# Folded attention: both masked halves on VectorE, the scaling of all four heads on ScalarE

## The chip, the cores and the metric

The kernel runs on one core of one Trainium2 chip. The core has a matrix engine (TensorE, in the profile PE for matmuls and PEld for its weight loads), VectorE (DVE), ScalarE (ACT), GpSimd (POOL), and SyncE (SP), which issues the DMA transfers. The metric is the device time of one execution in microseconds, as the median of several runs. Each engine works through its own instructions in the order of the program; engines wait for each other on semaphores.

## The reference

One decoder layer on a sequence of 1024 positions and a width of 1024, in float32. Part of it is a sliding-window attention with 16 query heads on 2 key/value heads and a learned sink per head, which enters the softmax but has no value:

```python
qb = q.reshape(B, N, C, Hkv, G, d)          # N = 8 blocks of C = 128, G = 8, d = 64
kb = jnp.concatenate([kp[:, :-1], kp[:, 1:]], axis=2)   # the block before, and this one
scores = jnp.einsum('bnqhgd,bnkhd->bnhgqk', qb, kb) * (d ** -0.5)
mask = (rel >= 0) & (rel < WINDOW) & (key_pos >= 0)     # WINDOW = 128
scores = jnp.where(mask, scores, -1e30)
m = jnp.maximum(jnp.max(scores, axis=-1, keepdims=True), sink)
e = jnp.exp(scores - m)
probs = e / (jnp.sum(e, axis=-1, keepdims=True) + jnp.exp(sink - m))
out = jnp.einsum('bnhgqk,bnkhd->bnqhgd', probs, vb)
```

Around it stand the combined input projection, a chunkwise retention with four heads, two sigmoid gates, an output projection and a SwiGLU block of 2816 columns, with RMS norms between.

## The kernel before, in words

Matmuls keep nearly float32 precision by splitting each operand into a high part (`h`) and the rest (`l`) and adding three products (hi·hi, hi·lo, lo·hi): ScalarE writes the high part, VectorE the difference.

The attention is *folded*. With a window of 128, query i of a block needs the keys after i in the block before and the keys up to i in its own: together always 128. So the two halves of scores are laid over each other in one 128×128 matrix, chosen by a mask. The values then need two products: the folded probabilities times one of the two value blocks, and the probabilities under the mask times the difference of the two value blocks (`vdf`).

The work is cut into 32 units: four groups g of four query heads, times eight blocks b. For a unit, `u_scores` makes the score matmuls (L477, L478, into PSUM tiles `s`), copies and chooses the halves (L482 on ScalarE, L483 on VectorE), takes the row minimum (L485; scores are negated), exponentiates on ScalarE with a row sum (L493; each has a second, short instruction that reads the sum), takes the reciprocal (L496, VectorE) and multiplies the probabilities of heads 1 and 3 on ScalarE (L499) and of heads 0 and 2 on VectorE (L501). GpSimd copies the sink column into the score tile (L469). `u_transpose` transposes the four heads on TensorE (L509, `pT`), writes the high part `ph` (L511, ScalarE) and the low part `pl` (L512, VectorE), and, for every block but the first of a group, multiplies both by the mask on GpSimd (L519, `qh` and `ql`). `u_values` runs the value matmuls on ph, pl, qh and ql (L530), brings the two halves of the heads together in `tm` (L533 and L534 on ScalarE, L535 and L536 on VectorE) and splits the result into hi and lo (L538, L539).

`ph`, `pl`, `qh` and `ql` have one buffer each (`bufs=1`), the score tile two.

Between units, dense matmuls fill TensorE: the query projections of the next group (`quad_q`, L159 to L161 with `aq`, with splits of weights in L419 and L420, and the rotation on VectorE and ScalarE in L427 to L446) and gate columns (`gate`, the same lines with `acc_g`, weights split in L132 and L135, tanh in L545). The loop hands out 8 steps of three matmuls a unit:

```python
            if i > 0:
                u_transpose(i - 1)
            if i < NU:
                u_scores(i)
            fl.step((i + 1) * left // (NU + 1) - i * left // (NU + 1))
            if i > 0:
                u_values(i - 1)
```

The order in which instructions really stand is not that of this text. A scheduler of the framework takes the instructions as they are traced, with its own assumed cost for each on its engine, and sets the order of every engine's queue from that. A changed engine or cost therefore moves the rows of all engines in the stage. What follows the attention (retention, output, SwiGLU) is not touched in the code.

## Time and profile before

| | us |
|---|---|
| Median of three runs (1582.39 to 1582.92) | 1582.56 |
| Profiled execution, its own time | 1584.13 |
| Its span, first to last instruction | 1582.3 |
| TensorE busy (matmuls) | 1555.2, 98% |
| VectorE busy | 1013.4, 64% |
| ScalarE busy | 719.6, 45% |
| GpSimd busy | 452.8, 29% |
| Mean granted TensorE clock | 0.996 |

Folded attention with its fill stands between about 95 and 342 us of the span. A row of the table by stage gives the stage, its length, then the busy time of PE, PEld, DVE, ACT and POOL with the number of instructions, then the granted clock as a share of the full one, the share of DMA engines in use, and GB/s. A row of the waits reads: engine, tile and line that waited, the engine, tile and line that released it, total us, times, longest. A row of the timeline gives start, duration, engine, line, operation, out<-in, and in brackets the idle time of the engine just before and who ended it. Matmuls are pipelined and their shown ends are modelled, so that consecutive rows overlap; the distance of two starts is what a matmul costs.

### The profile page before, as it was taken

What the parts mean: (1) busy time and instruction counts of PE and PEld (TensorE: products, weight loads), DVE (VectorE), ACT (ScalarE), POOL (GpSimd) and SP (SyncE); (2) the same over time, 40 slices, a digit from 0 to 9 for tenths busy, and PEclk for the clock granted to TensorE, in tenths of its full rate; (3) what the DMA queues carried; (4) which work ended last, traced back from release to release, by engine and by line L of the source; (5) the groups of instructions that cost most, each with busy time, mean ns of one, the idle gap of its engine ahead of it and who ended that gap; (6) DMA issues with size and microseconds to landing.
All of it is one profiled execution on the core that took longest, in us unless ns stands there. A gap on an engine that the chain in (4) does not pass through costs nothing.

```text
span 1582.3 us, 20602 instructions
## 1 busy us (share of the span) xinstructions
PE 1555.2 (98%) x7323; PEld 1288.0 (81%) x7323; DVE 1013.4 (64%) x1676; ACT 719.6 (45%) x1492; POOL 452.8 (29%) x376
## 2 busy tenths in 40 slices
PE   9998899999999999999999999999999999999998
PEld 8876777888888888888888888888888888888886
DVE  6458869677758663688656879544444444678656
ACT  6356777753333334544323366333333333344445
POOL 2013334320035541000021122655555555100001
PEclk9999899999999999999999999999999999999999
DMA  6563466350274543755455502333333333762233
GB/s 214 160 166 94 158 220 195 101 170 31 74 256 143 154 150 133 272 194 174 142 202 185 210 1 72 108 106 110 109 102 100 102 109 109 280 256 83 99 102 125
DMA packets 152581, 228.43 MB, mean 144 GB/s; under 512 B 9307, under 2 KB 81821, under 8 KB 150942
## 3 DMA queue, kind: packets, MB, share of 16 engines
q1 hardware_dynamic: 152476, 227.10, 43.6%
q8 instruction: 58, 0.95, 0.2%
q14 instruction: 45, 0.37, 0.1%
q10 hardware_dynamic: 2, 0.00, 0.0%
HBM read 152.36 MB, written 69.99 MB: 141 GB/s over the span
## 4 chain that ended last, share of the span: by engine, by line
PE 89%; DVE 4%; ACT 4%; POOL 2%; issue 1%; DMA 1%; POOLq 0%; DVEq 0%; ACTq 0%; SPq 0%
PE fA L1549 15%; PE fB L1549 8%; PE dA L1851 7%; PE wA L873 7%; PE dxP L1851 6%; PE fC L1549 4%; PE wB L873 3%; PE wo L1383 3%; PE va L718 3%; PE acc_g L159 2%; PE acc_g L160 2%; PE acc_g L161 2%; PE woP L1383 2%; PE vP L718 2%; PE acc_ba L159 2%; PE acc_ba L160 2%
## 5 line engine op out<-in xcount | busy, mean ns | idle before, releaser
L1851 PE MATMUL dA<-dwP,daP 128*128 128x512 f32 x528 | 120.6, 389 | 0.0
L1851 PEld LDWEIGHTS dA<-dwP,daP 128*128 128x128 f32 x528 | 99.1, 188 | 20.7 <-DVE dwP L135 0.2
L1851 PE MATMUL dxP<-dwP,daP 128*128 128x512 f32 x396 | 90.2, 389 | 0.0
L1851 PEld LDWEIGHTS dxP<-dwP,daP 128*128 128x128 f32 x396 | 74.3, 188 | 15.4
L159 PE MATMUL acc_g<-h,wh_g 128*128 128x512 f32 x192 | 77.2, 402 | 1.4 <-ACT wh_g L132 1.4
L160 PE MATMUL acc_g<-h,wh_g 128*128 128x512 f32 x192 | 76.2, 397 | 0.0
L161 PE MATMUL acc_g<-h,wl_g 128*128 128x512 f32 x192 | 75.8, 396 | 0.0
L1624 POOL TENSOR_TENSOR xf<-xf 128x512 f32<-128x512 f32 x40 | 62.4, 1561 | 30.7 <-issue 28.9
L469 POOL COPY sc<-nsink 128x4 f32<-128x4 f32 x32 | 11.5, 359 | 191.1 <-PE pT L509 157.8
L1555 POOL TENSOR_TENSOR xf<-xf 128x512 f32<-128x512 f32 x33 | 47.3, 1434 | 59.0 <-ACT xf L1557 26.9
L1756 POOL TENSOR_TENSOR rs_f<-tot,mhalf 128x1 f32<-128x1 f32 x8 | 4.8, 606 | 205.4 <-DVE tot L1753 205.4
L493 ACT ACTIVATE sc<-sc,nm 128x129 f32<-128x129 f32 x128 | 50.4, 396 | 26.6 <-DVE nm L485 20.7
L135 DVE TENSOR_TENSOR dwP<-wd,dwP 128x512 fp32r<-128x512 f32 x77 | 52.9, 687 | 5.3 <-ACT dwP L132 5.3
L1038 POOL TENSOR_TENSOR grs<-gve,mhalf 128x2 f32<-128x2 f32 x16 | 11.2, 701 | 145.5 <-DVE gve L1036 145.5
L587 POOL TENSOR_TENSOR wr_f<-wr_f 128x512 f32<-128x512 f32 x20 | 30.6, 1532 | 76.8 <-DVE t_10P L135 8.6
L132 ACT CAST dwP<-wd 128x512 fp32r<-128x512 f32 x77 | 47.4, 616 | 9.3 <-PE dA L1851 7.1
L587 POOL TENSOR_TENSOR wr_wp<-wr_wp 128x512 f32<-128x512 f32 x10 | 16.1, 1611 | 121.7 <-DVE w0P L135 103.6
L159 PE MATMUL acc_bb<-ay,wh_bb 128*128 128x512 f32 x128 | 50.9, 399 | 0.0
L132 ACT CAST daP<-daP 128x512 fp32r<-128x512 f32 x42 | 26.0, 621 | 54.2 <-PE dxP L1851 26.7
L159 PE MATMUL aq<-h,wh_aq 128*128 128x512 f32 x128 | 50.4, 394 | 0.0
L160 PE MATMUL acc_bb<-ay,wh_bb 128*128 128x512 f32 x128 | 50.3, 393 | 0.0
L160 PE MATMUL aq<-h,wh_aq 128*128 128x512 f32 x128 | 50.3, 393 | 0.0
(841 smaller groups left out, 4485.7 us busy)
## 6 DMA issues: line engine op xcount, KB each, us to landing
act_d<-xf SPq DMA_DIRECT2D x77, 256.0 KB, 2.1
daP<-act_d SPq DMA_DIRECT2D x21, 512.0 KB, 3.7
q_d<-stg SPq DMA_DIRECT2D x8, 1024.0 KB
q<-q_d SPq DMA_DIRECT2D x32, 256.0 KB, 6.7
ay_d<-q SPq DMA_DIRECT2D x8, 1024.0 KB
ay<-ay_d SPq DMA_DIRECT2D x4, 2048.0 KB, 13.9
wr_daP<-act_d SPq DMA_DIRECT2D x14, 512.0 KB, 6.5
wr_g<-in_w_in SPq DMA_DIRECT2D x12, 512.0 KB, 4.5
```

The lines of the kernel that those rows point to most:

```text
L132: nc.scalar.copy(hi, raw)
L135: return nc.vector.tensor_tensor(out=lo, in0=raw, in1=f32(hi), op=ALU.subtract)
L159: nc.tensor.matmul(pt, hi[:, k, :], xh, start=(k == 0), stop=False)
L160: nc.tensor.matmul(pt, hi[:, k, :], xl, start=False, stop=False)
L161: nc.tensor.matmul(pt, lo[:, k, :], xh, start=False, stop=(k == 7))
L493: nc.scalar.activation(sc[:, j, 0:P + 1], sc[:, j, 0:P + 1], AF.Exp, scale=-1.0, bias=nm[:, j:j + 1], accum_out=den[:, j:j + 1])
L718: nc.tensor.matmul(vbanks[pr][tt], x_[:, c], w[:, u, :], start=(fresh and k + z == 0), stop=(k == 3 and z == 2), skip_group_check=not fresh)
L873: nc.tensor.matmul(pt, o[:, w, k, :], v, start=(first and k + z == 0), stop=(k == 3 and z == 2), skip_group_check=not first)
L1383: nc.tensor.matmul(bank, v[:, q + u, k, c], w[y][:, k % 2, :], start=(first and z == 0), stop=(last and z == 2), skip_group_check=not tracked)
L1549: nc.tensor.matmul(pt, o[:, w, k, :], v, start=(first and n == 0), stop=(n == 11), skip_group_check=not first)
L1624: nc.gpsimd.tensor_tensor(out=o, in0=a, in1=b, op=op)
L1851: nc.tensor.matmul(banks[tt], a[:, u, c], w[:, v, :], start=(fresh and f + z == 0), stop=(f == NP - 1 and z == 2), skip_group_check=not fresh)
```

## The change

The product with the mask (both halves, 56 instructions over 28 units) is issued on VectorE instead of GpSimd, and all four heads of a unit are scaled by ScalarE, where VectorE did two of them. GpSimd keeps only the sink column's copy.

```diff
             rd = tiny.tile([P, 4], F32, tag="rd", name=f"rd{g}{b}")
             nc.vector.reciprocal(rd, den)
             for j in range(4):
-                if j % 2:
-                    nc.scalar.activation(sc[:, j, 0:P], sc[:, j, 0:P], AF.Copy, scale=rd[:, j:j + 1])
-                else:
-                    nc.vector.tensor_scalar(out=sc[:, j, 0:P], in0=sc[:, j, 0:P], scalar1=rd[:, j:j + 1],
-                                            scalar2=None, op0=ALU.mult)
+                nc.scalar.activation(sc[:, j, 0:P], sc[:, j, 0:P], AF.Copy, scale=rd[:, j:j + 1])
...
                 for t, src in (("qh", ph), ("ql", pl)):
                     o = w1.tile([P, 512], F32R, tag=t, bufs=1, name=f"{t}{g}{b}")
-                    nc.gpsimd.tensor_tensor(out=o.rearrange("p (j q) -> p j q", j=4),
+                    nc.vector.tensor_tensor(out=o.rearrange("p (j q) -> p j q", j=4),
                                             in0=f32(src).rearrange("p (j q) -> p j q", j=4), in1=mk, op=ALU.mult)
```

Lines behind the first hunk stand four lines earlier in the changed kernel: L509 becomes L505, L512 L508, L519 L515, L530 L526, L535 and L536 L531 and L532.

The scheduler sets other orders. Three places follow; a number in a name is that of the tile, and a tile keeps its number. First TensorE, group 0, block 5: the value matmuls of the unit (`pv_1449`) among the projections of the next group. Before:

```order
L159 MATMUL aq_1518<-h_111,wh_aq_1420 128x512
L160 MATMUL aq_1518<-h_111,wh_aq_1420 128x512
L530 MATMUL pv_1449<-ph_1369,vev 128x512
L161 MATMUL aq_1518<-h_111,wl_aq_1421 128x512
L159 MATMUL aq_1518<-h_111,wh_aq_1420 128x512
L160 MATMUL aq_1518<-h_111,wh_aq_1420 128x512
L530 MATMUL pv_1449<-pl_1370,vev 128x512
L530 MATMUL pv_1449<-qh_1373,vdf 128x512
L530 MATMUL pv_1449<-ql_1375,vdf 128x512
L477 MATMUL s_1488<-kst,q_641 128x256
```

In the changed kernel:

```order
L526 MATMUL pv_1449<-ph_1369,vev 128x512
L160 MATMUL aq_1518<-h_111,wh_aq_1420 128x512
L161 MATMUL aq_1518<-h_111,wl_aq_1421 128x512
L526 MATMUL pv_1449<-pl_1370,vev 128x512
L161 MATMUL aq_1598<-h_110,wl_aq_1423 128x512
L159 MATMUL aq_1598<-h_110,wh_aq_1422 128x512
L526 MATMUL pv_1449<-qh_1373,vdf 128x512
L160 MATMUL aq_1598<-h_110,wh_aq_1422 128x512
L161 MATMUL aq_1598<-h_110,wl_aq_1423 128x512
L159 MATMUL aq_1598<-h_111,wh_aq_1422 128x512
L526 MATMUL pv_1449<-ql_1375,vdf 128x512
```

pl, qh and ql stood directly behind each other; now two or three fill matmuls stand between any two of them.

The same unit on VectorE, around its low part `pl_1370`. Before:

```order
L501 TENSOR_SCALAR sc_1297<-sc_1297,rd_1321 128x128 x2
L535 TENSOR_TENSOR tm_1357<-pv_1352,tm_1357 64x256
L536 TENSOR_TENSOR tm_1357<-pv_1352,tm_1357 64x256
L539 TENSOR_TENSOR q_641<-tm_1357,q_641 128x2x128
L512 TENSOR_TENSOR pl_1370<-pT_1364,ph_1369 128x512
L483 COPY_PREDICATED sc_1377<-amask,s_1391 128x2x128
```

In the changed kernel:

```order
L531 TENSOR_TENSOR tm_1357<-pv_1352,tm_1357 64x256
L532 TENSOR_TENSOR tm_1357<-pv_1352,tm_1357 64x256
L508 TENSOR_TENSOR pl_1370<-pT_1364,ph_1369 128x512
L515 TENSOR_TENSOR qh_1373<-ph_1369,amask 128x512
L535 TENSOR_TENSOR q_641<-tm_1357,q_641 128x2x128
L515 TENSOR_TENSOR ql_1375<-pl_1370,amask 128x512
```

The two scalings are gone from this queue, the masks stand behind pl, and L539 of the unit before (now L535) has moved from ahead of pl to between the masks.

Last, TensorE in group 1, where the projections of the next group are through and the first gate column follows: the transposes `pT_1801` of one unit, behind the scores `s_1828` of the next. Before:

```order
L478 MATMUL s_1828<-kst,q_641 128x256
L509 MATMUL pT_1801<-ident,sc_1720 128x128 x4
L477 MATMUL s_1898<-kst,q_641 128x256
L478 MATMUL s_1898<-kst,q_641 128x256
L477 MATMUL s_1898<-kst,q_641 128x256
L478 MATMUL s_1898<-kst,q_641 128x256
L477 MATMUL s_1908<-kst,q_641 128x256
L530 MATMUL pv_1869<-ph_1806,vev 128x512
```

In the changed kernel:

```order
L478 MATMUL s_1828<-kst,q_641 128x256
L526 MATMUL pv_1789<-ph_1712,vev 128x512
L159 MATMUL acc_g_0_1850<-h_110,wh_g_1846 128x512
L526 MATMUL pv_1789<-pl_1713,vev 128x512
L160 MATMUL acc_g_0_1850<-h_110,wh_g_1846 128x512
L159 MATMUL acc_g_1_1933<-h_110,wh_g_1846 128x512
L526 MATMUL pv_1789<-qh_1716,vdf 128x512
L160 MATMUL acc_g_1_1933<-h_110,wh_g_1846 128x512
L526 MATMUL pv_1789<-ql_1718,vdf 128x512
```

Where the transposes followed the scores directly, the value matmuls of the unit before and gate matmuls now stand; `pT_1801` comes fifteen gate matmuls further down, each of its transposes but the last two alone.

## The prediction

> **What bounds the kernel now.** I read the page's slices first, then a table by stage, then TensorE's waits in the attention stage, then single stretches of the timeline. In the table the columns are the stage and its length, then busy time and count of PE, PEld, DVE, ACT and POOL, then the granted clock, the DMA share and GB/s.

> ```profile
> 95.00:342.00 247.00, 229.80 (x1129) 183.35 (x1128) 184.13 (x434) 177.22 (x559) 87.10 (x86) 0.98 0.50 154
> 95.00:140.00 45.00, 41.11 (x206) 31.43 (x205) 35.21 (x85) 30.67 (x101) 12.48 (x13) 1.00 0.56 158
> 140.00:170.00 30.00, 26.51 (x131) 19.62 (x131) 26.47 (x63) 22.26 (x74) 11.71 (x13) 1.00 0.29 91
> 170.00:184.00 14.00, 10.30 (x34) 7.81 (x33) 12.37 (x22) 9.12 (x28) 3.20 (x3) 0.63 0.80 202
> 342.00:1582.30 1240.30, 1232.27 (x5658) 1024.37 (x5656) 779.14 (x1158) 501.32 (x863) 355.84 (x266) 1.00 0.42 140
> ```

> Folded attention is the stage from 95 to 342 us. There PE stands idle for 247.0 − 229.8 = 17.2 us; behind it only 8.0 us are idle in 1240. So the change can win or lose only in this stage, most of it before 184 us, and what it wins there is kept, because PE is full behind it. The two longest waits of the weight loads and of the matmuls in the stage (total us, times, longest):

> ```profile
> PEld pv L530 <- POOL ql L519: 11.9, 11, 1.4
> PEld pT L509 <- ACT sc L499: 5.2, 10, 1.0
> ```

> ```profile
> PE pv L530 <- POOL ql L519: 8.0, 11, 1.0
> PE pT L509 <- DVE sc L501: 2.9, 4, 1.7
> ```

> GpSimd's low half ql is the largest. One such wait as it runs, with the chain ahead of it:

> ```profile
> 141.16 0.27 PE L509 MATMUL pT<-ident,sc 128*128 128x128 f32 x1
> ...
> 142.21 0.69 DVE L512 TENSOR_TENSOR pl<-pT,ph 128x512 fp32r<-128x512 f32 x1 [0.18 <-ACT ph L511]
> ...
> 143.45 1.27 POOL L519 TENSOR_TENSOR ql<-pl,amask 128x512 fp32r<-128x512 f32 x1
> 143.54 0.50 PE L530 MATMUL pv<-qh,vdf 128*128 128x512 f32 x1
> 144.77 0.50 PE L530 MATMUL pv<-ql,vdf 128*128 128x512 f32 x1 [0.73 <-POOL ql L519]
> ```

> pl ends at 142.90, but GpSimd is still on qh and starts ql at 143.45. The value matmul on ql starts 1.23 us after the one on qh, where two 512-column matmuls otherwise start 0.23 apart (102.81 to 103.04, in rows below). The loss is 1.00 us, and the weight loads' column gives it: 11.9 / 11 = 1.08. The matmul's own column says 0.73, since a matmul's shown length reaches into the gap. So I price these waits at 11.9 us, with 8.0 as the lower bound.

> **The change, part by part. (a) The masks.** 56 operations leave GpSimd for VectorE. The durations are min/median/max in ns:

> ```profile
> L519 POOL TENSOR_TENSOR qh<-ph,amask x28: 1275/1301/1722, 111.4 to 337.2; 128x512 fp32r<-128x512 f32 x28
> L519 POOL TENSOR_TENSOR ql<-pl,amask x28: 1267/1476/1737, 112.8 to 338.4; 128x512 fp32r<-128x512 f32 x28
> L438 DVE TENSOR_TENSOR stg<-q,atab x8: 664/688/1778, 62.4 to 254.0; 128x512 f32<-128x512 f32 x8
> L483 DVE COPY_PREDICATED sc<-amask,s 128x256 f32<-128x256 uint32 x56 | 23.1, 438 | 1.4 <-ACT sc L482 1.0
> ```

> No trace row has this mask product on VectorE. L438 is a product of the same size with two inputs, undisturbed 0.69 us; L512 above takes as long. The other bound is L483, which also reads a repeated mask: 0.438 us for 256 elements, so 0.88 for 512. I take 0.69, because shape and operation are those of L438. Back to back VectorE starts the next one about 0.61 later (142.21 + 0.69, with the overlap of 0.08 that consecutive rows show), so qh and ql are ready 1.2 us after pl instead of up to 1.9.

> From the start of the last transpose the old chain needs 144.77 − 141.16 = 3.6 us until the ql matmul. The new one needs 142.90 − 141.16 + 2 × 0.61 = 3.0 us, and 3.35 where the order of VectorE puts L539 (about 0.35) between. The room that TensorE's own order leaves between those two instructions, counted in rows at 0.23, 0.12 and 0.11 us, was under 3.6 in nine of the 28 masked units; the shortages add up to 10.4 us, which is the 11.9 measured. In the new order the matmuls on ph, pl, qh and ql stand two or three fill matmuls apart, and only three units are short: 0.34, 0.74 (two weight splits L420 stand ahead of the masks) and 0.35 us, and a few ph and pl matmuls by 0.6 together. So 11.9 becomes about 2.0: **−9.9 us**. Bounds: −6 (8.0 − 2.0) and −11.9.

> **(b) The scaling.** 64 products leave VectorE, 64 come to ScalarE.

> ```profile
> L501 DVE TENSOR_SCALAR sc<-sc,rd x64: 269/282/1378, 101.1 to 333.7; 128x128 f32<-128x128 f32 x64
> 172.29 0.69 ACT L499 ACTIVATE sc<-sc,rd 128x128 f32<-128x128 f32 x2
> L499 ACT ACTIVATE sc<-sc,rd x64: 384/390/407, 101.0 to 333.8; 128x128 f32<-128x128 f32 x64
> ```

> Two in a row take 0.69, one takes 0.39, so each further one costs 0.30. The four now run in series: the last is ready 0.60 later in each unit. The new order answers that: most transposes stand singly, 90 alone against 9 before. That looks dear and is not:

> ```profile
> 102.13 0.60 PE L509 MATMUL pT<-ident,sc 128*128 128x128 f32 x4
> 102.49 0.48 PE L160 MATMUL acc_g<-h,wh_g 128*128 128x512 f32 x1
> 102.81 0.39 PE L161 MATMUL acc_g<-h,wl_g 128*128 128x512 f32 x1
> 103.04 0.39 PE L159 MATMUL acc_g<-h,wh_g 128*128 128x512 f32 x1
> ...
> 141.18 0.47 PE L160 MATMUL aq<-h,wh_aq 128*128 128x512 f32 x1
> 141.50 0.40 PE L161 MATMUL aq<-h,wl_aq 128*128 128x512 f32 x1
> ```

> Four together take 0.36 until the next matmul starts, and that one holds its follower 0.32 instead of 0.23: 0.45 in all, 0.11 each. The single one at 141.16 takes 0.02, and its successor again 0.32: also 0.11. Splitting costs nothing. The room from a unit's last score matmul to its first transpose is 5.7 us in most units after 190 us, with hardly a wait; in the new order it is mostly 7 to 9, more than the 0.6 of the series. I take **0** for (b); without that room it is 0.6 per unit.

> **(c) The hole at 170 us.**

> ```profile
> 170.22 0.28 PE L478 MATMUL s<-kst,q 128*128 128x256 f32 x1
> 172.17 0.30 PE L509 MATMUL pT<-ident,sc 128*128 128x128 f32 x1 [1.68 <-DVE sc L501]
> 172.75 0.69 PE L509 MATMUL pT<-ident,sc 128*128 128x128 f32 x3 [0.27 <-ACT sc L499]
> ...
> 177.69 0.79 PE L159 MATMUL acc_g<-h,wh_g 128*128 128x512 f32 x1 [1.41 <-ACT wh_g L132]
> 178.28 0.63 PE L160 MATMUL acc_g<-h,wh_g 128*128 128x512 f32 x1
> 178.70 0.63 PE L159 MATMUL acc_g<-h,wh_g 128*128 128x512 f32 x1
> ```

> Here the fill has run out: scores, four transposes and the next scores follow directly. Two scores start 0.12 apart, so the gap before the first transpose is 1.95 − 0.12 = 1.8 us and that before the second 0.58 − 0.11 = 0.5. In the new order nineteen gate and four value matmuls stand between those scores and these transposes, so both gaps, 2.3 us, should go. What waits for wh_g (1.4) stays, and ph comes late there, because four scalings and L443, L445 and L538 stand ahead of it on ScalarE. I take **−2.0**, with bounds −2.3 and 0.

> Right behind the hole the granted clock is 0.63 over 14 us, which is half speed for about 10.3 us (14 × 0.37 / 0.5). PE was idle for about 2 of them; in the other 8.2 matmuls start 0.43 apart instead of 0.23, a loss of 8.2 × 0.47 = 3.8 us. If the hole is filled, I expect the drop to go: **−3.7**, or 0 if it stays.

> [...]

> **(d) What the queues carry.** VectorE in the stage: 184.1 − 19.3 (L501) + 56 × 0.61 = 199 us, and ScalarE 177.2 + 64 × 0.30 = 196, in a stage of some 235. From 95 to 170 us it is tighter: VectorE was busy for 61.7 of 75. Against that, VectorE's slow rows lose their cause. These lasted far over their 0.69 while GpSimd was on a mask:

> ```profile
> L444 DVE TENSOR_TENSOR stg<-stg 128x512 fp32r<-128x512 f32 x6 | 6.7, 1110 | 0.4 <-ACT stg L443 0.4
> L501 DVE TENSOR_SCALAR sc<-sc,rd 128x128 f32<-128x128 f32 x64 | 19.3, 342 | 0.7
> ```

> From L444 6 × (1.11 − 0.69) = 2.5 us come back; with its like on L438, L440, L442 and L446 I estimate 6. So VectorE ends near 193 of 235, 82%. Some of its work will come late for TensorE, behind masks that run first; I take **+4.0**, the middle between 0 (the room counted above holds everywhere) and +9 (all that VectorE gains in load, 34.2 − 19.3 − 6, lands on TensorE).

> [...]

> **The sum**: −9.9 + 0 − 2.0 − 3.7 + 4.0 = −11.6. The profiled execution took 1584.13 us, 1.8 over its span; its span would become 1570.7 and its time 1572.5. The three runs have a median of 1582.56, 1.6 below that execution, so the forecast is 1571.0.

> **Rivals.** *The clock still drops* (wh_g and ph leave gaps of 1.4 and about 1 in that place): 1571.0 + 3.7 = 1574.7. For it: the weights are late in both orders. *VectorE takes GpSimd's place*: tm of the previous unit (L535, L536), then pl, qh and ql run in one queue, and between 95 and 170 us it is above 80% full. (d) is then at its bound and the clock drop stays: −9.9 − 2.0 + 9 = −2.9, 1579.7. Against it: the room in the new order was counted with these rows in between. *Slower, by ScalarE's series*: where the fourth scaling ends behind its transpose's place, a unit pays 0.60, and the exponentials and ph queued behind the scalings are late with it. From 17 of the 32 units on this eats (a), as 17 × 0.60 = 10.2; with 24 units and nothing of (c) it is −9.9 + 14.4 = +4.5, 1587. For it: L499 already holds the weight loads of pT for 5.2 us. Against it: rooms of 5.7 us were enough with the queues as they were, and they grow by 1.3 or more where the series adds 0.6. *Nothing moves*: GpSimd was not the cause, ql is late because pl is, and PE waits the same on VectorE: 1582.5. Against it: in the timeline pl was ready 0.55 before GpSimd took it.

> **How the numbers follow.** Forecast 0.45, clock rival 0.27, VectorE rival 0.15, ScalarE rival 0.08, nothing 0.05. The likeliest alone spans 1566 to 1575. The range for 8 in 10 goes from 1562 (−20.6: (a) at −11.9, (c) at −2.3 and −3.7, (d) at 0 is −17.9, and 2 to 3 us more if other waits behind GpSimd's go too) to 1581 (the VectorE rival and a little of the next). A measurement here can tell about 0.2% or 3.2 us from no change, so faster means under 1579.4: 0.45 + 0.27 + 0.08 of the VectorE rival = 0.80; same, 0.07 of it and most of the last, 0.11; slower 0.09.

> **What would show it.** In the changed profile the mask rows should stand on VectorE, 56 of 0.69 us; the waits of pv should have no GpSimd row and only some 2 to 4 us behind VectorE; L438, L444 and L446 should have no row above 0.75; the transposes should wait on ScalarE for no more than 5 us; the granted clock should be 1.00 from 160 to 190. PE's idle time between 95 us and the end of the stage should be 6 to 9 us. Wrong would be: mask rows of 0.88, waits of pv for VectorE near 10, or transposes that wait in most units.

## The result, and the profile after

The changed kernel takes 1567.52 us (median of four, 1566.55 to 1567.63) against 1582.74 us for the kernel before (median of four, 1582.39 to 1585.12): ratio 0.990 with a 95% interval of 0.988 to 0.991. A second measurement of the same kernel, beside other runs of the one before, gave 1567.91 us and 0.990 (0.989 to 0.992). It is faster by 15 us, where 11.6 were forecast; the forecast of 1571.0 is 3.5 us too long.

The table by stage of the changed kernel, with the columns of the table before. The stage ends some 16 us earlier, so its last row but one runs to 326 us.

```profile
95.00:140.00 45.00, 44.59 (x235) 36.36 (x233) 39.39 (x94) 39.61 (x133) 2.47 (x6) 1.00 0.63 179
140.00:170.00 30.00, 27.23 (x133) 20.39 (x133) 27.76 (x65) 27.10 (x86) 2.81 (x5) 1.00 0.49 156
170.00:184.00 14.00, 14.00 (x75) 11.47 (x74) 11.37 (x27) 11.62 (x41) 0.38 (x2) 1.00 0.42 146
95.00:326.00 231.00, 224.36 (x1125) 180.01 (x1124) 185.83 (x428) 193.00 (x623) 10.40 (x30) 1.00 0.52 164
326.00:1564.80 1238.80, 1231.09 (x5651) 1023.03 (x5650) 780.39 (x1157) 501.40 (x862) 355.10 (x266) 1.00 0.42 140
```

The gain lies in the stage. TensorE now idles for 6.6 of its 231 us (17.2 of 247 before), from 170 to 184 us it has no gap and its full clock, and behind the stage 7.7 us are idle in 1239, as before. Its matmul waits and its longest weight-load waits there (total us, times, longest):

```profile
PE pT L505 <- ACT sc L498: 2.1, 4, 1.2
PE pv L526 <- DVE tm L532: 1.7, 3, 0.8
PE pv L526 <- DVE qh L515: 0.9, 2, 0.7
PE acc_g L159 <- ACT wh_g L132: 0.6, 2, 0.5
PE pv L526 <- ACT ph L507: 0.5, 1, 0.5
```

```profile
PEld pT L505 <- ACT sc L498: 9.8, 31, 1.6
PEld pv L526 <- ACT ph L507: 3.0, 6, 0.9
PEld pv L526 <- DVE qh L515: 2.8, 6, 0.9
```

No row names GpSimd any more; the value matmuls now wait for tm, qh and ph, a little each. The masks on VectorE, and two of its rows that had been stretched (min/median/max in ns):

```profile
L515 DVE TENSOR_TENSOR qh<-ph,amask x28: 679/682/686, 110.1 to 322.4; 128x512 fp32r<-128x512 f32 x28
L515 DVE TENSOR_TENSOR ql<-pl,amask x28: 682/684/686, 110.7 to 323.0; 128x512 fp32r<-128x512 f32 x28
L438 DVE TENSOR_TENSOR stg<-q,atab x8: 660/684/693, 60.0 to 237.5; 128x512 f32<-128x512 f32 x8
L444 DVE TENSOR_TENSOR stg<-stg x8: 682/692/693, 66.7 to 242.0; 128x512 fp32r<-128x512 f32 x8
```

All 56 masks take 0.68, where 0.69 was predicted, and L438 no longer has its longest of 1.78, nor L444 its mean of 1.11: as the prediction said, neither has a row above 0.75.

### What each place in the stage loses

Waits of weight loads and of matmuls each tell only part: behind the scaling, the loads of pT above wait 9.8 us in all and its matmuls 2.1. So I took the distances of successive matmul starts, from the first score matmul to the first of the retention, and subtracted the undisturbed ones: 0.228 us for 512 columns (the median of this stage in the kernel before), 0.118 for 256 (there, the mean of six in a row from 169.51 to 170.22 us), and 0.11 for a transpose (last section). What is left is lost, and is booked on the matmul that came late. What lies inside a stretch of half clock is booked there.

| kernel | stage | waits, all | pv | pT | s | acc_g | lost to half clock |
|---|---|---|---|---|---|---|---|
| before | 270.7 | 29.1 | 14.8 | 7.4 | 3.0 | 2.0 | 3.6 |
| changed | 255.7 | 17.4 | 5.7 | 5.1 | 1.1 | 1.9 | 0 |
| changed, measured again | 255.6 | 17.3 | 5.7 | 5.1 | 1.0 | 1.9 | 0 |
| masks to VectorE only | 253.9 | 14.7 | 2.8 | 5.1 | 1.8 | 2.0 | 1.3 |
| scaling to ScalarE only | 272.0 | 32.3 | 15.8 | 8.8 | 3.2 | 1.3 | 1.5 |
| masks and one scaling in four on VectorE | 252.8 | 14.8 | 2.9 | 5.3 | 1.6 | 1.3 | 0 |
| masks and all scalings on VectorE | 259.2 | 18.7 | 3.9 | 6.9 | 1.7 | 2.1 | 2.4 |
| only ql to VectorE | 265.1 | 23.6 | 8.3 | 7.7 | 2.2 | 2.6 | 3.6 |

The stage less waits and clock loss is 237.9 to 238.3 us in every row. All these kernels have the same 1232 matmuls there, and since each is counted at its undisturbed distance, the differences stand under waiting and clock. The change wins 15.0 us in the stage: 9.1 at pv, 2.3 at pT, 1.9 at s, 3.6 of clock; gaps too small to list take the rest back. The two profiled executions differ by 17.5, since the one of before also began its stage 2.4 us later; that part is no effect of the change (last section).

### The profile page after: what moved, and what is told of

Same layout as the page of the kernel before. It is cut to its first block, busy times and chain, and to the rows that moved or that the text cites. A ratio compares the mean times of both kernels' runs of the same rounds, so it can differ in the third digit from the quotient of the medians.

```text
span 1564.8 us, 20561 instructions
## 1 busy us (share of the span) xinstructions
PE 1549.0 (99%) x7323; PEld 1284.4 (82%) x7323; DVE 1016.2 (65%) x1668; ACT 735.2 (47%) x1556; POOL 375.3 (24%) x320
## 4 chain that ended last, share of the span: by engine, by line
PE 88%; ACT 6%; DVE 4%; issue 1%; DMA 1%; SPq 0%; POOL 0%; POOLq 0%; ACTq 0%; DVEq 0%
PE fA L1545 15%; PE fB L1545 8%; PE dA L1847 7%; PE wA L869 7%; PE dxP L1847 6%; PE fC L1545 4%; PE wB L869 3%; PE wo L1379 3%; PE va L714 3%; PE woP L1379 2%; PE vP L714 2%; PE acc_ba L161 2%; PE acc_ba L159 2%; PE acc_ba L160 2%; PE acc_bb L159 2%; PE acc_bb L160 2%
## 5 line engine op out<-in xcount | busy, mean ns | idle before, releaser
L159 PE MATMUL acc_g<-h,wh_g 128*128 128x512 f32 x192 | 76.9, 401 | 0.6 <-ACT wh_g L132 0.6
L160 PE MATMUL acc_g<-h,wh_g 128*128 128x512 f32 x192 | 76.4, 398 | 0.0
L161 PE MATMUL acc_g<-h,wl_g 128*128 128x512 f32 x192 | 76.4, 399 | 0.0
L493 ACT ACTIVATE sc<-sc,nm 128x129 f32<-128x129 f32 x128 | 50.4, 397 | 19.3 <-DVE nm L485 15.4
L132 ACT CAST daP<-daP 128x512 fp32r<-128x512 f32 x42 | 26.0, 621 | 55.0 <-PE dxP L1847 26.7
L132 ACT CAST dwP<-wd 128x512 fp32r<-128x512 f32 x77 | 47.4, 616 | 8.8 <-PE dA L1847 6.6
L159 PE MATMUL acc_bb<-ay,wh_bb 128*128 128x512 f32 x128 | 51.2, 400 | 0.0
L160 PE MATMUL aq<-h,wh_aq 128*128 128x512 f32 x128 | 50.6, 395 | 0.0
L161 PE MATMUL aq<-h,wl_aq 128*128 128x512 f32 x128 | 50.5, 395 | 0.0
L159 PE MATMUL aq<-h,wh_aq 128*128 128x512 f32 x128 | 50.3, 393 | 0.0
L160 PE MATMUL acc_bb<-ay,wh_bb 128*128 128x512 f32 x128 | 50.3, 393 | 0.0
L161 PE MATMUL acc_bb<-ay,wl_bb 128*128 128x512 f32 x128 | 50.1, 391 | 0.0
L159 PE MATMUL acc_ba<-yg,wh_ba 128*128 128x512 f32 x128 | 49.9, 390 | 0.0
```

Source lines behind the costliest of these rows:

```text
L132: nc.scalar.copy(hi, raw)
L159: nc.tensor.matmul(pt, hi[:, k, :], xh, start=(k == 0), stop=False)
L160: nc.tensor.matmul(pt, hi[:, k, :], xl, start=False, stop=False)
L161: nc.tensor.matmul(pt, lo[:, k, :], xh, start=False, stop=(k == 7))
L493: nc.scalar.activation(sc[:, j, 0:P + 1], sc[:, j, 0:P + 1], AF.Exp, scale=-1.0, bias=nm[:, j:j + 1], accum_out=den[:, j:j + 1])
```

## The experiments

### The two parts alone

First the masks alone go to VectorE, with the scaling split as before:

```diff
-                    nc.gpsimd.tensor_tensor(out=o.rearrange("p (j q) -> p j q", j=4),
+                    nc.vector.tensor_tensor(out=o.rearrange("p (j q) -> p j q", j=4),
```

> Only the masks move to VectorE; heads 0 and 2 are still scaled there. Theory (the masks are the cause): nearly all of the 15 us comes, 1567 to 1571 us; pv's matmuls wait for no GpSimd row and for less than 6 us in all. Rival (freeing VectorE of the scaling is needed, its queue would be too full): pl, qh and ql come late behind the 64 scalings, and half the gain or less is left, 1575 us or more.

It took 1564.44 us, ratio 0.988 (0.986 to 0.990). Its executions run from 1563.6 to 1565.6, those of the changed kernel from 1566.6 to 1568.9: the masks alone are about 3 us better than the whole change, and better than I had expected. In the two profiled executions the stage differs by 1.8 us only (253.9 against 255.7), since the one with the masks alone lost 1.3 us to half clock.

```profile
95.00:326.00 231.00, 225.79 (x1132) 182.23 (x1131) 200.86 (x495) 176.13 (x560) 10.93 (x30) 0.99 0.53 164
```

In this row of the table by stage VectorE is busy for 200.9 of 231 us, 15 more than with the whole change, and yet TensorE loses only 2.8 us at pv. The waits of VectorE point to a reason. First the longest of the changed kernel, then the same one here:

```profile
DVE tm L531 <- ACT tm L530: 25.8, 23, 2.7
```

```profile
DVE tm L535 <- ACT tm L534: 12.2, 16, 1.4
```

ScalarE copies one half of the heads to tm, VectorE adds the other. With four scalings in ScalarE's queue VectorE stands 13.6 us longer at this addition, and what is behind it in its queue, the masks among it, stands too. `pv` has one buffer, so the next value matmuls also wait for the addition itself. That fits TensorE's waits: the changed kernel has 1.7 us of pv behind tm and 0.9 behind qh (above), and with the masks alone neither row is there. The two longest are then:

```profile
PE pv L530 <- ACT ph L511: 1.2, 3, 0.6
PE pT L509 <- DVE sc L501: 1.2, 1, 1.2
```

Then the scaling alone, with the masks left on GpSimd:

```diff
-                if j % 2:
-                    nc.scalar.activation(sc[:, j, 0:P], sc[:, j, 0:P], AF.Copy, scale=rd[:, j:j + 1])
-                else:
-                    nc.vector.tensor_scalar(out=sc[:, j, 0:P], in0=sc[:, j, 0:P], scalar1=rd[:, j:j + 1],
-                                            scalar2=None, op0=ALU.mult)
+                nc.scalar.activation(sc[:, j, 0:P], sc[:, j, 0:P], AF.Copy, scale=rd[:, j:j + 1])
```

> Only the scaling moves to ScalarE; the masks stay on GpSimd. Theory (the masks are the cause): ql still holds pv for about 11 us, nothing is won; the series on ScalarE adds between 0 and 4, so 1581 to 1587 us. Rival (the scaling carries the gain, because transposes no longer wait for a VectorE that GpSimd slows): 1576 us or less.

1585.4 us, ratio 1.001 (1.000 to 1.002): nothing is won, and perhaps 1 or 2 us are lost. The weight loads' longest waits:

```profile
PEld pv L526 <- POOL ql L515: 15.5, 15, 1.4
PEld pT L505 <- ACT sc L498: 12.5, 30, 1.6
```

GpSimd's wait stays and grows from 11.9 to 15.5. The gain belongs to the masks alone; the scaling takes some of it back.

### Half of the masks

```diff
-                    nc.gpsimd.tensor_tensor(out=o.rearrange("p (j q) -> p j q", j=4),
+                    (nc.gpsimd if t == "qh" else nc.vector).tensor_tensor(out=o.rearrange("p (j q) -> p j q", j=4),
```

> From the kernel before: only ql moves to VectorE, qh stays on GpSimd, the scaling stays split. The chain to ql is then pl and one product (0.6 us after pl). Theory (the chain to ql is what counts): as good as both masks on VectorE within 4 us, 1563 to 1569 us, less the slowing of ql and other VectorE rows by GpSimd's qh. Rival (GpSimd beside VectorE costs more than the shorter chain wins): 1572 us or more.

1577.78 us, ratio 0.996 (0.994 to 0.997). pv falls from 14.8 to 8.3 us. Half the masks give about half of the gain at pv; the clock fell to half twice in this order, for 3.6 us as in the kernel before. I had expected 1563 to 1569 us and missed; the time lies where the rival put it, at 1572 or more. What the rival gave as its reason is not shown by that: the weight loads of pv waited for qh on GpSimd for 2.3 us, but for pl on VectorE for 3.4 and for ph on ScalarE for 3.0, and how much of this is GpSimd beside VectorE and how much the new order stays open.

### How much scaling ScalarE bears

Both of these have the masks on VectorE. In the first all four scalings are on VectorE too (`nc.vector.tensor_scalar` for every j). In the second VectorE keeps one:

```diff
-                if j % 2:
+                if j:
```

> Both masks on VectorE as in the change, and VectorE also scales all four heads (four times about 0.2 us behind each other, where ScalarE takes four times 0.3). Theory (the series on ScalarE is what makes the change 3 us worse than the masks alone): the transposes wait less than behind ScalarE, and the time is that of the masks alone within 3 us, 1562 to 1568 us. Rival (VectorE becomes the bound with 64 products more): 1571 us or more, and pv waits for pl, qh and ql.

> Both masks on VectorE as in the change, but of a unit's four scalings the first stays on VectorE and three go to ScalarE (the change: four; masks to VectorE alone: two and two; all on VectorE: none). Theory (the change lost about 3 us by ScalarE's longer series, because ph and tm queue behind it): the time lies between 1564.4 (two and two) and 1567.5 (four), about 1566, with pv's waits between 2.8 and 5.7 us. Rival (the 3 us come from the order that the planner happens to find and not from the series): the time lies outside of 1563.5 to 1568.5, and pv's waits do not follow the number of scalings.

With none on ScalarE the time is 1570.96 us, ratio 0.992 (0.990 to 0.994); with three it is 1565.00, ratio 0.989 (0.988 to 0.991). So by the number of scalings on ScalarE: none 1570.96, two 1564.44, three 1565.00, four 1567.5. With none the theory's 1562 to 1568 did not come; the time stands at the edge of the rival's 1571, but what waits most for VectorE there are the transposes, where the rival had named pv. All scalings on VectorE, the stage and TensorE's longest wait:

```profile
95.00:326.00 231.00, 223.86 (x1109) 177.33 (x1108) 209.06 (x550) 155.06 (x491) 11.79 (x30) 0.99 0.52 162
```

```profile
PE pT L506 <- DVE sc L498: 3.5, 4, 2.1
```

Here VectorE is at 90% of the stage and the transposes wait for it, up to 2.1 us at a time. Three on ScalarE and one on VectorE, VectorE's longest wait:

```profile
DVE tm L535 <- ACT tm L534: 10.4, 21, 1.7
```

I had expected a middle value for three, 1566 with 2.8 to 5.7 us at pv. Both lie inside what I had allowed, but at the end next to two: 2.9 at pv, and VectorE waits for tm no longer than with two. So by pv and tm the loss does not grow evenly with the series; it comes with the fourth scaling. The times say less: against the kernel before, each beside its own runs, the ratios are 0.988, 0.989 and 0.990 for two, three and four, with intervals that overlap. Each of these kernels has an order of its own, and how much of the 3 us is the length of the series, and how much the order that the planner found with it, stays open.

### TensorE's order and the engines apart

Two kernels hold TensorE's matmuls in an order given by a table, up to the retention; the other engines' queues are planned anew around it. The first has the change's engines with the order of before, the second the engines of before with the change's order:

```diff
+PE_ORDER = """
...
+    for a, b in zip(names, names[1:]):
+        tc.add_manual_dep(by[b], a, mybir.DependencyInfo(mybir.DependencyClass.NoSync, mybir.DependencyReason.DATA),
+                          reason="pe_order")
```

> The changed kernel's engines, but TensorE's matmuls are held in the order of the kernel before (the other engines are scheduled anew around it). Theory A (the shorter chain carries the gain): the nine short units need 3.0 to 3.35 us instead of 3.6 but have 1.75 to 3.08 of room, so pv's waits fall from 14.8 to about 7 us; the hole and the slow clock stay: 1574 to 1577 us. Theory B (the order carries it): next to nothing is won, 1580 us or more. If the shorter chain carried all of it: 1570 us or less.

> The engines of the kernel before, but TensorE's matmuls are held in the order of the changed kernel. Theory A (the shorter chain carries the gain): the masks on GpSimd are late also here, at most 5 us are won, 1577 us or more. Theory B (the order carries it: more room between pl, qh and ql, and fill in the hole): the rooms are short by about 3 us in all against the old need of 3.6 us, the clock does not drop, and most of the gain comes with the old engines: 1567 to 1573 us.

Both theories missed. The change's engines in the old order take 1602.83 us, ratio 1.012 (1.011 to 1.014), slower than either kernel; the old engines in the new order 1588.12, ratio 1.003 (1.002 to 1.004). First the one, then the other:

```profile
PEld pT L532 <- ACT sc L525: 27.3, 65, 2.9
```

```profile
PEld pv L561 <- ACT ph L542: 10.5, 11, 1.8
PEld pv L561 <- POOL ql L550: 8.9, 15, 1.1
```

In the old order four scalings on ScalarE come too late for the transposes, 65 times; the room that the new order gives them is what makes them cheap. In the new order with the old engines ql is still waited for, and ph is late on top. In these two runs neither the order nor the engines win anything by themselves: the fill that the planner puts between the value matmuls was of use only where the masks came from VectorE. But the first run mixes two things. Counted as in the table above, pv lost about 10 us there instead of 14.8, and pT about 25 instead of 7.4. So the shorter chain helped pv in the old order too, somewhat less than theory A had said, and the scaling on ScalarE took more back at the transposes. The masks alone were not run in the old order, so how the gain divides between the chain and the order stays open.

### GpSimd's work beside VectorE's

The first try added work to the changed kernel that nobody reads: GpSimd repeats both masked products of a unit into a scratch tile, in eight pieces.

```diff
+                for src in (ph, pl):
+                    for j in range(4):
+                        junk = gt.tile([P, P], F32, tag="junk", bufs=1, name=f"junk{g}{b}")
+                        nc.gpsimd.tensor_tensor(out=junk, in0=f32(src)[:, j * P:(j + 1) * P], in1=mk[:, j], op=ALU.mult)
```

> The changed kernel, and GpSimd in addition makes the same masked halves once more, into a scratch tile that nobody reads (eight 128-column products a unit). Nobody waits for them except the next ph and pl, which wait until they are read. Theory (what the change wins is the time in which ql is ready, and that GpSimd leaves VectorE's rows alone is a small part): VectorE's two-input rows L438, L444 and the masks themselves reach 1 us and more again, and 2 to 6 us are lost against the changed kernel: 1569 to 1574 us. Rival (the gain is that GpSimd is quiet): most of the 15 us is lost, 1578 us or more.

1589.02 us, ratio 1.004 (1.002 to 1.005): 21 us more than the change, far outside the theory's span and inside the rival's. The groups of VectorE's masks (busy us, mean ns of one), and the weight loads that waited for them:

```profile
L515 DVE TENSOR_TENSOR ql<-pl,amask 128x512 fp32r<-128x512 f32 x28 | 26.4, 944 | 0.0
L515 DVE TENSOR_TENSOR qh<-ph,amask 128x512 fp32r<-128x512 f32 x28 | 25.2, 902 | 0.0
```

```profile
PEld pv L530 <- DVE ql L515: 11.5, 20, 1.4
PEld pv L530 <- DVE qh L515: 6.3, 13, 1.0
```

VectorE's masks are slowed from 0.68 to over 0.90. But the planner set a new order here too, and GpSimd also held ph and pl longer (eight pieces of 0.61 us a unit), which have one buffer each. The second try takes both away. TensorE's order is held, the queues of the other engines keep their order as well, and GpSimd multiplies constants, five products of 128 columns behind each sink column:

```diff
+        for u, nxt in zip(sinks, sinks[1:]):
+            last = u
+            for n in range(5):
+                i = nc.gpsimd.tensor_tensor(out=junk, in0=ident, in1=ident, op=ALU.mult).ins
+                behind(i, last)
+                last = i
+            behind(nxt, last)
```

> Everything of the change, with TensorE's matmuls held in the change's own order, and every instruction of VectorE, ScalarE and SyncE in its order too. Added is work that nobody reads: behind each unit's sink column GpSimd makes five products of the identity with itself, 128 columns each, into a scratch tile, about 155 in the stage. No other engine waits for them. Theory (GpSimd's two-input work slows VectorE's two-input work, so that taking it away from GpSimd was worth something beside the masks' own time): VectorE's mask rows of 0.68 grow to between 0.75 and 0.95 on the mean, with the longest over 1.0, waits of pv behind VectorE grow from about 5 to between 8 and 12 us, and the time is 1569 to 1574 against 1567.5 for the change. Rival (the earlier run with GpSimd repeating the masks lost its 21 us by contention alone): 1578 or more here too. Second rival (VectorE is slowed but has the room): mask rows grow, the time stays within 1 us of the change.

1573.07 us, ratio 0.994 (0.993 to 0.996), 5.5 us over the change, inside the theory's span; the masks grew to a mean of 0.74, a little less than it said. The stage, and the groups of the masks:

```profile
95.00:326.00 231.00, 222.67 (x1104) 174.70 (x1103) 189.72 (x420) 190.46 (x618) 81.96 (x175) 1.00 0.52 161
```

```profile
L548 DVE TENSOR_TENSOR ql<-pl,amask 128x512 fp32r<-128x512 f32 x28 | 20.9, 746 | 0.0
L548 DVE TENSOR_TENSOR qh<-ph,amask 128x512 fp32r<-128x512 f32 x28 | 20.7, 741 | 0.0
```

GpSimd is busy for 82 us, about as in the kernel before. Nobody waits for its products, no order is changed, and VectorE's own busy time grows from 185.8 to 189.7 us in the same window. TensorE's waits grow by 5.1 (pv 2.1, pT 1.3, acc_g 1.0). No engine has a wait for GpSimd in the stage, so its sink columns were not late either. So GpSimd's products cost time here, 5.5 us, although no result of theirs is needed. The kernel before had about as much of such work on GpSimd, so a part of what the masks win, of about this size by this run, may come from VectorE's rows running undisturbed and not from the shorter chain; no run takes the two apart. The rival, that contention alone explains the first try's 21 us, would have given 1578 or more here and did not come; this load was lighter, though. What the first try lost beyond these 5.5 us, by its heavier load on GpSimd, its order and its buffers, is not taken apart.

### The hole and the clock

Eight matmuls of 512 columns fill the hole at 170 us in the kernel before. A table holds TensorE's order as above, and in the trace every other instruction of every engine stands where it stood; the transposes overwrite the result.

```diff
+            if u == 10:
+                for _ in range(8):
+                    nc.tensor.matmul(pt, H[0][:, 0, 0:P], H[0][:, 0, 0:512], start=True, stop=True)
```

> The kernel before, with every instruction of every engine in its own order, and eight matmuls of 512 columns added on TensorE between the scores and the transposes where TensorE stood for 1.8 us at 170 us; their result is overwritten by the transposes and nothing else changes. Their work, 8 x 0.23 = 1.8 us, fits the gap. Theory (the clock falls to half because of the gaps just ahead of it): no period of half speed from 170 to 184 us, the stage loses 3.6 us of slow clock, and the time is about 1579.5 to 1580.5 against 1583.5 for the kernel before. Rival (the drop does not hang on these gaps: it comes at its time, or from all the waiting before): the half-speed period is there all the same, and the time is within 1 us of before or up to 0.5 us longer.

1582.52 us against 1582.76, ratio 1.000 (0.999 to 1.001). The 3.6 us were not won. The timeline at the hole:

```profile
170.19 0.28 PE L517 MATMUL s<-kst,q 128*128 128x256 f32 x1
170.31 2.00 PE L549 MATMUL pT<-h 128*128 128x512 f32 x8
172.16 0.30 PE L551 MATMUL pT<-ident,sc 128*128 128x128 f32 x1
...
176.59 0.53 PE L198 MATMUL acc_g<-h,wh_g 128*128 128x512 f32 x1 [1.41 <-ACT wh_g L171]
176.93 0.62 PE L199 MATMUL acc_g<-h,wh_g 128*128 128x512 f32 x1
```

Rows of the table by stage for the stretch of half clock, first in the kernel before, then two rows here:

```profile
173.20:183.40 10.20, 8.45 (x24) 6.53 (x24) 10.13 (x15) 5.66 (x14) 3.20 (x3) 0.50 0.80 202
```

```profile
160.00:176.90 16.90, 14.47 (x74) 11.21 (x73) 15.12 (x31) 12.54 (x37) 5.08 (x5) 1.00 0.64 201
176.90:183.70 6.80, 6.39 (x15) 4.17 (x14) 6.80 (x11) 3.03 (x8) 1.28 (x1) 0.50 0.59 122
```

The hole is full, and the clock did stay at 1.00 past 173.2, where it had fallen before. But behind the next gap, the wait for wh_g, it fell at 176.9, for 6.8 us instead of 10.2. The loss to half clock fell from 3.6 to 2.6, and the waits for the gate's weights grew by the same 1.0, since TensorE came to them earlier. The theory was right that the drop hangs on the gaps just ahead, since filling one moved it from 173.2 to 176.9, and wrong that this one made it alone. In the changed kernel both are gone: its row from 170 to 184 us has no gap, and its wait for wh_g is 0.6 in two times.

## Why the prediction was right

**What bounds the kernel.** Right: the gain lies in the stage, and what is won there is kept.

**(a) The masks, −9.9.** Right in mechanism, and the experiments show it: with the masks alone on VectorE pv falls from 14.8 to 2.8 us, −12.0. Whether GpSimd's lateness was the cause is settled by the pair of single parts: with only the scaling moved ql is waited for as before. That excludes the rival "nothing moves", and the rival "VectorE takes GpSimd's place" as well, since pv waits for qh and ql on VectorE in few units. The price was a little low, as pv lost more than the 11.9 of the ql rows: qh, pl and ph of the same units were late as well. (The count of rooms gave 10.4, which is near the 11.9 but not the same, as the prediction has it.) And the account has one cause where the runs show two: some of the gain, up to the 5.5 us of the run with idle products on GpSimd, may be VectorE's freedom from GpSimd, which the prediction had only as busy time in (d).

**(b) The scaling, 0.** This step failed. Its working looked at the transposes and found room for them, and there it was right: pT loses 5.1 us with two or four scalings on ScalarE. The loss stands at pv, 5.7 instead of 2.8 us, and by the waits it comes another way: tm on ScalarE stands behind the scalings, VectorE stands at its part of tm for 25.8 us instead of 12.2, and the next pv waits for that and for the masks behind it. That chain is read from the waits of kernels with different orders; no run isolates it. The rival on ScalarE's series named the queue on ScalarE, with the exponentials and ph in it, but not tm, and the sum had nothing. Measured: about +3 us in the time, from 1564.44 to 1567.5, and +2.9 at pv. That rival's 1587 did not come: it needed 17 units that pay at the transposes. The transposes' weight loads do wait for ScalarE more than the 5 us that were named as a sign, 9.8 in 31 times and 21 of the 32 units, so "transposes that wait in most units" came too. But the starts behind them lose no more than with the masks alone, 5.1 us in both; the sign was badly chosen.

**(c) The hole, −2.0, and the clock, −3.7.** Both sizes came out: pT −2.3, clock −3.6. For pT that is the sum of the places: the hole's 2.3 us went, and elsewhere gaps came and went, one of 1.4 us at 155 us among the new. That the clock stayed was partly luck: with the masks alone a gap of 1.3 us at about the same time was followed by a drop of 3.4 us. And the reason given for the clock was half of it. Filling the hole does not keep the clock in the kernel before: it fell all the same, at 176.9 us, behind the wait of 1.41 us for wh_g, which the clock rival had named. That wait shrank to 0.6 in all in the new order, which the prediction did not see; it had said that this wait stays.

**(d) VectorE's fuller queue, +4.0.** Mis-sized, and by its mechanism: the runs show nothing of VectorE's load as such. With VectorE at 200.9 us of 231, more than the change makes it, pv loses 2.8 us in all. One part of the sum was wrong by rows that could be read: I estimated that 6 us of stretched VectorE time come back, and it was 12.5. The six rotation lines gave 8.7, and a line that I had not looked at, L539 (L535 now), gave 3.8. Before, and after:

```profile
L539 DVE TENSOR_TENSOR q<-tm,q 128x256 fp32r<-128x256 f32 x31 | 16.7, 539 | 0.8 <-ACT q L538 0.7
```

```profile
L535 DVE TENSOR_TENSOR q<-tm,q 128x256 fp32r<-128x256 f32 x31 | 12.9, 417 | 3.0 <-ACT q L534 3.0
```

So VectorE ended at 185.8 us of 231 and not at 193 of 235. The rest of the step, that lateness on VectorE lands on TensorE, is seen only in the run with all scalings on it, busy for 209.1 of 231 us (90%): its time is 6.5 us worse than with half of them. In the changed kernel VectorE's lateness does cost TensorE time, but through its waits for ScalarE's tm, which is (b).

**The sum.** −12.0 for the masks at pv, +2.9 for the scaling there, −5.9 for hole and clock, 0 for (d): −15.0, which is what the stage won, where −9.9 + 0 − 5.7 + 4.0 = −11.6 stood. (The 1.9 us won at s and what small gaps took back are left out; they cancel.) Two errors, (a) too small and (d) too large, outweighed the missing price of (b). That the forecast is only 3.5 us off is thus in part luck: its errors of 2.1, 4.0 and 2.9 us do not all point the same way.

## What to carry to other kernels

Take the two halves of a change apart before accepting it: here the masks alone, or with three of four scalings on ScalarE, give 1564.4 to 1565.0 us, better than both kernels; by the waits, the second half made a queue longer that other work stands in. When an operation is moved, look at everything behind it on its new engine, not only at who reads its result; and count what its old engine slowed, by comparing min and median with the mean of each row (L438 of the kernel before: 0.66 and 0.69 against 0.87 us). Where a planner sets the order, judge an assignment of engines only with the order that fits it: held in the other's order, each of the two here was slower than the kernel before.

## What the runs showed of the hardware

**The start of the program has two lengths.** Of the kernel before, and of the changed one:

```profile
4.96 3.78 PE L267 MATMUL g<-wk 1*128 1x512 f32 x4
```

```profile
4.78 1.98 PE L267 MATMUL g<-wk 1*128 1x512 f32 x4
```

These four matmuls take 3.77 or 3.78 us in four of the thirteen profiles, and 1.98 to 2.33 in the others, whatever the variant. The four late ones all begin their stage at 97.7 us, the others between 95.2 and 97.1. Fifteen executions of the kernel before in one measurement fall into two groups, 1581.7 to 1582.8 and 1583.7 to 1584.9 us. That the start is what parts them is inferred, since there is one trace of this kernel and not fifteen; either way two profiles are better compared stage by stage than by their spans.

**GpSimd's products stretch some of VectorE's rows.** With 82 us of them in the stage the masks went from 0.68 to 0.74 on the mean, and with 128 us, in another order, to 0.90 (qh) and 0.94 (ql). Of the six L438 rows of the stage in the kernel before, the three that no mask of GpSimd overlapped took at most 0.69 us, the longest of the others 1.78. Not every row is stretched: L512 took at most 0.69 in all of its 32, and a mask ran beside 25 of them.

**Transposes cost the same alone and together**: 0.11 us each, by the median of 26 groups of four in the kernel before (0.111) and of 90 single ones in the changed kernel (0.115), with what the next matmul is held up counted in.
